# Twelve small products of attention's query and key norms, issued one by one between main products

## The chip, the core and the metric

The kernel runs on one core of a Trainium2 chip. Its time is what the device takes for one execution, in microseconds (us); the median of three runs before the change was 2003.21 us, the lowest 1998.88, the highest 2009.31.

The core's engines work side by side: TensorE (PE in the profile, its weight loads PEld) multiplies matrices, VectorE (DVE), ScalarE (ACT) and GpSimd (POOL) do the elementwise work, SyncE (SP) issues transfers. Each takes its instructions in the order of its own queue, and waits where it needs something that another has not finished.

## The reference

One layer of an encoder over 768 tokens (512 in a grid of 8 x 64, 256 in one of 4 x 64) of 2048 channels, in float32. Cut to what matters here:

```python
h = _rms(x, norm_g) * (1 + scl) + shift
proj = h @ w_in                      # 2048 x 10240
pool_u, pool_z, q, k, v, attn_z, g_pool, g_attn = split(proj)
pool_y = _pool_mixer(pool_u) * silu(pool_z)
q = _rms(q.reshape(B, S, 16, 64), q_norm_g)     # x * rsqrt(mean(x * x) + eps) * g, by head
k = _rms(k.reshape(B, S, 16, 64), k_norm_g)
attn_y = _neighbourhood_attention(q, k, v, rpb) * silu(attn_z)
merged = sigmoid(g_pool) * (pool_y @ w_pool_up) + sigmoid(g_attn) * (attn_y @ w_attn_up)
y = x + gate * (merged @ w_o)
```

The change is in the two lines for `q` and `k`: the sum of x * x over the 64 channels of each head, for every token.

## The kernel before, in words

**The main products.** Nearly all of TensorE's work is the projections. Channels lie on the partitions, tokens along the row. A weight and an operand are each split into a high and a low part, and one product becomes three main products in `steps`, line 493: high by high, high by low, low by high, each a load of 128 x 128 weights and 384 columns of the operand. A generator, `steps`, issues them; after every second weight tile (six main products) it calls `tick`. The parts of the weights (`whi` from ScalarE, `wlo` from VectorE) are made three pieces ahead.

**The small work by ticks.** Everything else is put on a calendar: `at(step, fn)` files a function under a tick, and `tick` calls what is due, so that its instructions stand in each engine's queue right behind the main products issued so far. Attention runs in eight pairs of heads, 42 ticks apart, beside the main products of the second half of the projection. A pair has six units of queries; a unit makes its scores `s` (tick 0), adds the bias on VectorE (1), exponentials on ScalarE (3), transposes the values (`vt`, 5) and the probabilities (`pt`, 9), splits these into parts (`ph` by ScalarE, `pl` by VectorE, 10), and multiplies (`op`, 13).

**The norms** (`norms`, from line 540) come ahead of a pair's first unit. ScalarE squares the pair's keys and queries (`sq`, line 550, two tiles of 128 x 768). TensorE sums the squares over each head's 64 channels (`n`, line 556): twelve instructions, six for the keys and six for the queries, each with 128 tokens' squares as weights and two columns of ones as its operand. The trace shows each as two passes, so 24 a pair. VectorE adds the epsilon (`nx`, 564), ScalarE takes logarithm and exponential (`ny`, 567 and 568), VectorE does a Newton step (`ny`, 574), TensorE spreads the result over the channels (`yk`, 592), and VectorE scales the keys. The tile of the sums, the scores and `yk` take turns in one PSUM buffer (the tag `s`).

Of the kernel before, what the change touches and what calls it, by code (L numbers as in the profile page):

```python
# [16 lines left out]
P = 128  # L17
# [34 lines left out]
def encoder_layer(ctx: ExitStack, tc: tile.TileContext, xT, cT, w_ada2, w_ada4, b_ada, norm_g, w_in, pool_w,  # L52
                  pool_scale, qg, kg, rpb, rcnt, w_pu, w_au, w_o, yT):
    nc = tc.nc
    pe, act, dve, pool, sp = nc.tensor, nc.scalar, nc.vector, nc.gpsimd, nc.sync
# [13 lines left out]
    def slot(name, dt=F32):  # L69
        heap["live"] += 1  # L70
        heap["peak"] = max(heap["peak"], heap["live"])
        assert heap["live"] <= SLOTS, (name, heap)
        return slab.tile([P, 2, TH], dt, tag="slot", name=name, bufs=SLOTS)

    def free(n=1):
        heap["live"] -= n
# [17 lines left out]
    def flat(t):  # L94
        return t.rearrange("p h n -> p (h n)")
# [6 lines left out]
    blk1 = const.tile([P, P], F32, name="blk1")  # L102
# [45 lines left out]
    def at(step, fn):  # L148
        plan.setdefault(max(step, clock["now"] + 1), []).append(fn)
# [2 lines left out]
        at(clock["now"] + n, fn)  # L152

    chores = []
    back = []
    pace = {"kind": "pair", "task": 0, "chore": 0, "back": 0}
    EVERY = {"plain": 1, "drop": 2, "pair": 3}
# [16 lines left out]
    def tick():  # L174
        clock["now"] += 1
        while plan.get(clock["now"]):
            plan[clock["now"]].pop(0)()
        pump()
# [152 lines left out]
    def need(st, op, j):  # L331
        hurry["on"] = True
        while (op, j) not in st.ops:
            if tasks and room() >= tasks[0][0] and tasks[0][1]():
                tasks.pop(0)[2]()
            elif back and room() >= back[0][0] and back[0][1]():
                back.pop(0)[2]()
            else:
                assert behind, (st.name, op, j, heap, len(tasks), len(back))
                flush()  # L340
        hurry["on"] = False
        if behind and behind["of"] is st.ops[op, j]:
            flush()
# [44 lines left out]
    def prepare(upto):  # L388
        load_more()
        while st_["split"] < min(len(seq), upto):  # L390
            split_next()
            load_more()

    def bank():
        return ps_acc.tile([P, 512], F32, tag="acc", name="acc", bufs=4)
# [80 lines left out]
    def steps():  # L476

        for i, s in enumerate(seq):
            prepare(i + 1 + st_["ahead"])
            c = s["c"]  # L480
            pace["kind"] = "plain" if s["kind"] == "plain" else "drop" if s["drop"] else "pair"
            if s["kind"] == "pair":
                stt, n = s["set"], s["n"]
                for j in range(n):
                    need(stt, s["op"], j)
                if s["first"]:
                    c[s["bank"]] = bank()
                out = c[s["bank"]][:, :TH]
                for j in range(n):
                    mh, ml = stt.mov(s["op"], j)  # L490
                    wh, wl = s["hi"][:, j, :], s["lo"][:, j, :]
                    for k, (w, m) in enumerate(((wh, mh), (wh, ml), (wl, mh))):
                        pe.matmul(out, w, m, start=s["first"] and j == 0 and k == 0, stop=j == n - 1 and k == 2,  # L493
                                  skip_group_check=True)
                    if j == n - 1:
                        if s["drop"]:
                            stt.drop(s["op"])
                        if s["hook"]:
                            s["hook"]()
                    if j % 2:  # L500
                        tick()
                        yield
            else:
                if s["begin"]:
                    c["ps"] = s["banks"]() if s["banks"] else [bank()[:, :TH] for _ in range(2)]
                for j in range(s["n"]):
                    mov = s["mov"](s["k0"] + j)
                    last = s["end"] and j == s["n"] - 1
                    for k, (w, m) in enumerate(((s["hi"], 0), (s["hi"], 1), (s["lo"], 0))):
                        for h in range(2):  # L510
                            pe.matmul(c["ps"][h], w[:, j, :], mov[h][m], start=s["begin"] and j == 0 and k == 0,  # L511
                                      stop=last and k == 2, skip_group_check=True)
                    if last:
                        s["hook"](c["ps"])
                    tick()
                    yield
# [3 lines left out]
    def run(n):  # L520
        if stream["gen"] is None:
            stream["gen"] = steps()
        for _ in range(n):
            next(stream["gen"])
# [15 lines left out]
    def norms(p, start):  # L540


        at_ = state["pool"]
        c = {}

        def squares():
            for nm in "kq":
                assert clock["now"] >= state["done", nm, p] + 5, (p, nm, clock["now"], state["done", nm, p])
                c["s" + nm] = slot("sq")
                act.activation(flat(c["s" + nm]), flat(state[nm, p]), AF.Square)  # L550

        def sums():
            n2 = ps_aux.tile([P, 2, 512], F32, tag="s", name="n2")[:, 0, :]
            for i, nm in enumerate("kq"):
                for u in range(6):
                    pe.matmul(n2[:, 12 * i + 2 * u : 12 * i + 2 * u + 2], flat(c["s" + nm])[:, P * u : P * (u + 1)],  # L556
                              blk1[:, 0:P:64], start=True, stop=True)
            free(2)
            c["n2"] = n2[:, :24]

        def take():
            c["x"] = at_.tile([P, 24], F32, tag="nx", name="nx", bufs=2)
            c["y"] = at_.tile([P, 24], F32, tag="ny", name="ny", bufs=2)
            dve.tensor_scalar(c["x"], c["n2"], 64 * EPS, None, op0=ALU.add)

        def root():
            act.activation(c["y"], c["x"], AF.Ln)
            act.activation(c["y"], c["y"], AF.Exp, scale=-0.5)

        def newton():  # L570
            x, y = c["x"], c["y"]
            dve.tensor_tensor(x, x, y, op=ALU.mult)
            dve.scalar_tensor_tensor(x, x, -0.5, y, op0=ALU.mult, op1=ALU.mult)
            dve.scalar_tensor_tensor(y, x, 1.5, y, op0=ALU.add, op1=ALU.mult)
            state["yq", p] = y[:, 12:24]

        def high(nm):
            c[nm + "h"] = slot(nm + "h", F32R)
            act.copy(flat(c[nm + "h"]), flat(state[nm, p]))

        def low(nm):
            c[nm + "l"] = slot(nm + "l", F32R)
            dve.tensor_tensor(flat(c[nm + "l"]), flat(state[nm, p]), flat(c[nm + "h"]).bitcast(F32), op=ALU.subtract)
            free()
            state["parts", p] = c

        def spread():
            c["b"] = ps_aux.tile([P, 2, 512], F32, tag="s", name="yk")
            for u in range(6):
                for h in range(2):  # L590
                    src = c["y"][:, 2 * u + h : 2 * u + h + 1].to_broadcast([P, 64])
                    pe.matmul(c["b"][HALF[h], u // 3, P * (u % 3) : P * (u % 3 + 1)], src, ident, start=True, stop=True)  # L592

        def scaled():
            k = state["k", p]
            dve.scalar_tensor_tensor(k, k, gqk, c["b"][:, :, :TH], op0=ALU.mult, op1=ALU.mult)

        for n, fn in ((0, squares), (2, sums), (3, take), (4, root), (4, lambda: high("q")), (5, newton), (6, spread),
                      (6, lambda: low("q")), (7, scaled), (8, lambda: high("k")), (9, lambda: low("k"))):
            at(start - 11 + n, fn)  # L600

    def attention(p, start, pace):
        at_ = state["pool"]
        vparts = {}
        norms(p, start)

        def unit_(u):
# [749 lines left out]
```

## Time and profile before

| | |
|---|---|
| median of three runs | 2003.21 us |
| profiled execution | 1998.88 us |
| its span, first to last instruction | 1997.1 us |
| TensorE busy (products / loads) | 1910.8 / 1805.7 us |
| VectorE, ScalarE, GpSimd busy | 1353.2, 1028.5, 375.6 us |
| mean granted clock of TensorE | 0.982 of full |

A time in the text without another unit is in us; moments are counted from the span's start. TensorE is busy for 96% of the span, and the chain of work that ended last runs through it for 83%. The clock of TensorE has two levels in the rows, 1.00 (2.4 GHz) and 0.50 (1.2 GHz). Matmuls overlap in the records, since each lasts until its last column is out: to see what one costs, count the time from one start to the next.

### The profile page before, as it was taken

The numbers are of one execution on the slowest core, as the hardware profiler recorded it, in microseconds if no ns is written. First come the engines' busy times: TensorE is split into PE (matmuls) and PEld (weight loads), VectorE is DVE, ScalarE is ACT, GpSimd is POOL, SyncE is SP. The second block draws the span as 40 slices with busy tenths as digits, with TensorE's granted clock in tenths as the row PEclk, the third lists the DMA queues.
The fourth block names the chain that finished last, engine by engine and source line by source line (L and its number), as shares of the span: only waits on it lengthen the run. The fifth ranks groups of instructions, "written<-read, shape, count | busy, mean of one in ns | idle before, by whom it ended". The sixth has DMA issues, their size and how long they took to land.

```text
span 1997.1 us, 31988 instructions
## 1 busy us (share of the span) xinstructions
PE 1910.8 (96%) x11752; PEld 1805.7 (90%) x11752; DVE 1353.2 (68%) x2422; ACT 1028.5 (52%) x2224; POOL 375.6 (19%) x593
## 2 busy tenths in 40 slices
PE   3899999999999999999999999999998999898998
PEld 2788989898999998999888898889998999897997
DVE  5755555666656578866867787677765779776654
ACT  4433334444444344546666666666554556565553
POOL 0000000111300146511111111111143022222211
PEclk9999999999999999999999999999999999999999
DMA  9755556777753555566555665556799589898865
GB/s 357 247 204 190 195 195 209 265 256 246 245 194 120 165 157 130 136 184 152 164 151 149 159 176 140 151 149 173 170 326 364 191 290 255 250 301 242 244 184 148
DMA packets 129678, 410.61 MB, mean 206 GB/s; under 512 B 16369, under 2 KB 21489, under 8 KB 129521
## 3 DMA queue, kind: packets, MB, share of 16 engines
q0 software_dynamic: 61408, 194.28, 35.9%
q1 hardware_dynamic: 67104, 214.20, 32.0%
q8 instruction: 92, 1.51, 0.3%
q14 instruction: 66, 0.53, 0.1%
q10 hardware_dynamic: 1008, 0.09, 0.0%
HBM read 290.54 MB, written 117.96 MB: 205 GB/s over the span
## 4 chain that ended last, share of the span: by engine, by line
PE 83%; DVE 5%; DMA 4%; issue 3%; ACT 3%; POOL 1%; SPq 0%; ACTq 0%; POOLq 0%; DVEq 0%
PE acc L493 73%; PE adaacc L530 2%; PE op L715 2%; PE acc L511 1%; DVE wlo L382 1%; PE n L556 1%; DMA adaw<-in_w_ada_dram 1%; PE s L621 1%; PE pt L682 1%; DMA xrB<-xrB 1%; PE yk L592 1%; DVE wsum L405 0%; DMA merged_d<-o 0%; DMA mbB<-mbB 0%; ACT o L435 0%
## 5 line engine op out<-in xcount | busy, mean ns | idle before, releaser
L382 DVE TENSOR_TENSOR wlo<-wraw,whi 128x512 fp32r<-128x512 f32 (+1 forms) x352 | 244.0, 694 | 287.4 <-ACT whi L381 285.6
L382 DVE TENSOR_TENSOR wlo<-wsum,whi 128x512 fp32r<-128x512 f32 x440 | 315.3, 717 | 129.4 <-ACT whi L381 122.6
L381 ACT CAST whi<-wsum 128x512 fp32r<-128x512 f32 x440 | 272.9, 620 | 166.5 <-ACT whi L381 55.7
L493 PE MATMUL acc<-xbT,whi 128*128 128x384 f32 x1280 | 346.5, 352 | 4.5 <-ACT u L420 4.5
L493 PE MATMUL acc<-xaT,whi 128*128 128x384 f32 x1216 | 313.3, 338 | 0.5 <-DVE xaT L204 0.5
L381 ACT CAST whi<-wraw 128x512 fp32r<-128x512 f32 (+1 forms) x352 | 213.0, 606 | 89.7 <-PE acc L493 69.6
L493 PE MATMUL acc<-xbB,whi 128*128 128x384 f32 x960 | 251.0, 342 | 1.7 <-DVE o L839 1.7
L420 ACT COPY u<-acc 128x384 f32<-128x384 f32 x220 | 105.2, 478 | 285.1 <-PE acc L493 285.0
L493 PEld LDWEIGHTS acc<-xbT,whi 128*128 128x128 f32 x1280 | 231.2, 194 | 12.9 <-ACT u L420 6.5
L493 PE MATMUL acc<-xaB,whi 128*128 128x384 f32 x912 | 235.2, 338 | 0.0
L493 PEld LDWEIGHTS acc<-xaT,whi 128*128 128x128 f32 x1216 | 217.7, 188 | 15.3 <-issue 14.4
L493 PE MATMUL acc<-xbT,wlo 128*128 128x384 f32 x640 | 219.6, 343 | 0.2 <-DVE wlo L382 0.2
L493 PE MATMUL acc<-xaT,wlo 128*128 128x384 f32 x608 | 203.7, 335 | 0.0
L493 PEld LDWEIGHTS acc<-xbB,whi 128*128 128x128 f32 x960 | 169.1, 188 | 8.2 <-ACT o L914 2.0
L493 PEld LDWEIGHTS acc<-xaB,whi 128*128 128x128 f32 x912 | 163.1, 188 | 11.9 <-issue 9.9
L493 PE MATMUL acc<-xbB,wlo 128*128 128x384 f32 x480 | 161.1, 336 | 0.0
L493 PE MATMUL acc<-xaB,wlo 128*128 128x384 f32 x456 | 152.8, 335 | 0.0
L405 DVE TENSOR_TENSOR wsum<-wraw 128x512 f32<-128x512 f32 x220 | 152.5, 693 | 0.2 <-DMA wraw<-in_w_in_dram 0.2
L405 DVE TENSOR_TENSOR wsum<-wsum,wraw 128x512 f32<-128x512 f32 x220 | 151.3, 688 | 0.2
L493 PEld LDWEIGHTS acc<-xbT,wlo 128*128 128x128 f32 x640 | 123.9, 194 | 0.5 <-DVE wlo L382 0.5
L435 ACT ACTIVATE o<-acc 128x384 f32<-128x384 f32 x110 | 54.1, 492 | 128.1 <-PE acc L493 127.7
L852 POOL DMA_DIRECT2D part_d<-o x76 | 41.2, 542 | 397.9 <-ACT o L435 323.1
(244 smaller groups left out, 3558.2 us busy)
## 6 DMA issues: line engine op xcount, KB each, us to landing
wraw<-in_w_in_dram SPq DMA_DIRECT2D x160, 512.0 KB, 4.6
adaw<-in_w_ada_dram SPq DMA_DIRECT2D x96, 512.0 KB, 5.9
part_d<-o POOLq DMA_DIRECT2D x116, 384.0 KB, 3.9
wraw<-in_w_o_dram SPq DMA_DIRECT2D x32, 512.0 KB, 6.6
o<-part_d POOLq DMA_DIRECT2D x40, 384.0 KB, 4.8
xbT<-xbT POOLq DMA_DIRECT2D x32, 384.0 KB, 5.6
xrT<-xrT POOLq DMA_DIRECT2D x32, 384.0 KB, 7.4
xyT<-xyT POOLq DMA_DIRECT2D x32, 384.0 KB, 8.0
```

The costliest lines, as they stand in the source:

```text
L381: act.copy(hi[:, :n, :], raw)
L382: dve.tensor_tensor(lo[:, :n, :], raw, hi[:, :n, :].bitcast(F32), op=ALU.subtract)
L405: dve.tensor_tensor(t[:, :n, :], a, b, op=ALU.add)
L420: act.copy(t, c["a"][:, :TH])
L435: act.activation(c["o2"][:, 0, :], c["a"][:, :TH], AF.Copy, scale=-1.0)
L493: pe.matmul(out, w, m, start=s["first"] and j == 0 and k == 0, stop=j == n - 1 and k == 2, skip_group_check=True)
L511: pe.matmul(c["ps"][h], w[:, j, :], mov[h][m], start=s["begin"] and j == 0 and k == 0, stop=last and k == 2, skip_group_check=True)
L530: pe.matmul(acc[32 * j : 32 * (j + 1), :n], cs[:, kt, :], w[:, n * j : n * (j + 1)], start=kt == 0, stop=kt == KT - 1)
L556: pe.matmul(n2[:, 12 * i + 2 * u : 12 * i + 2 * u + 2], flat(c["s" + nm])[:, P * u : P * (u + 1)], blk1[:, 0:P:64], start=True, stop=True)
L592: pe.matmul(c["b"][HALF[h], u // 3, P * (u % 3) : P * (u % 3 + 1)], src, ident, start=True, stop=True)
L715: pe.matmul(op[:, :256], a, b, start=i == 0, stop=i == len(prods) - 1)
L852: pool.dma_start(part_d[f], flat(t))
```

## The change

The block of twelve instructions is broken up. `sums` no longer issues them: it files them in a list, `small`, and `steps` takes one from it behind the first and one behind the third of every three main products, until the list is empty. Six weight tiles, that is three ticks, use up the twelve. So that the results are there at the same tick as before, the squares and the sums begin three ticks earlier (14 ahead of the pair's first unit for the squares, 11 before), and `take`, `root`, `newton` and what follows stay at the tick they had. A new step, `summed`, gives the two slots of the squares back.

```diff
     chores = []
+    small = []
     back = []
...
                     for k, (w, m) in enumerate(((wh, mh), (wh, ml), (wl, mh))):
                         pe.matmul(out, w, m, start=s["first"] and j == 0 and k == 0, stop=j == n - 1 and k == 2,
                                   skip_group_check=True)
+                        if small and k != 1:
+                            small.pop(0)()
...
         def sums():
             n2 = ps_aux.tile([P, 2, 512], F32, tag="s", name="n2")[:, 0, :]
-            for i, nm in enumerate("kq"):
-                for u in range(6):
-                    pe.matmul(n2[:, 12 * i + 2 * u : 12 * i + 2 * u + 2], flat(c["s" + nm])[:, P * u : P * (u + 1)],
-                              blk1[:, 0:P:64], start=True, stop=True)
+            c["n2"] = n2[:, :24]
+
+            def one(i, nm, u):
+                pe.matmul(n2[:, 12 * i + 2 * u : 12 * i + 2 * u + 2], flat(c["s" + nm])[:, P * u : P * (u + 1)],
+                          blk1[:, 0:P:64], start=True, stop=True)
+
+            small.extend(lambda i=i, nm=nm, u=u: one(i, nm, u) for i, nm in enumerate("kq") for u in range(6))
+
+        def summed():
+            assert not small
             free(2)
-            c["n2"] = n2[:, :24]
...
-        for n, fn in ((0, squares), (2, sums), (3, take), (4, root), (4, lambda: high("q")), (5, newton), (6, spread),
-                      (6, lambda: low("q")), (7, scaled), (8, lambda: high("k")), (9, lambda: low("k"))):
-            at(start - 11 + n, fn)
+        for n, fn in ((0, squares), (2, sums), (6, summed), (6, take), (7, root), (7, lambda: high("q")), (8, newton), (9, spread),
+                      (9, lambda: low("q")), (10, scaled), (11, lambda: high("k")), (12, lambda: low("k"))):
+            at(start - 14 + n, fn)
```

On TensorE, around the sums of the third pair, this stood in the order before, from the transposes of one unit to the first main products behind the block (`xbT`, `xbB` are operands, the number is the buffer's):

```order
L682 MATMUL pt<-ident,p 128x128 x2
L682 MATMUL pt<-ident,p 64x128 x2
L493 MATMUL acc<-xbT_7088,whi 128x384 x2
L493 MATMUL acc<-xbT_7088,wlo 128x384
...
L493 MATMUL acc<-xbB_7153,whi 128x384 x2
L493 MATMUL acc<-xbB_7153,wlo 128x384
L660 MATMUL vt<-ident,o_9590 96x128
L660 MATMUL vt<-ident,o_9590 64x128
L556 MATMUL n_10538<-blk_84,sq 128x2 x12
L493 MATMUL acc<-xbT_5501,whi 128x384 x2
L493 MATMUL acc<-xbT_5501,wlo 128x384
```

And at the same place after it:

```order
L690 MATMUL pt<-ident,p 128x128 x2
L690 MATMUL pt<-ident,p 64x128 x2
L494 MATMUL acc<-xbT_7088,whi 128x384
L560 MATMUL n_10490<-blk_84,sq 128x2
L494 MATMUL acc<-xbT_7088,whi 128x384
L494 MATMUL acc<-xbT_7088,wlo 128x384
L560 MATMUL n_10490<-blk_84,sq 128x2
...
L494 MATMUL acc<-xbB_7153,wlo 128x384
L560 MATMUL n_10490<-blk_84,sq 128x2
L668 MATMUL vt<-ident,o_9590 96x128
L668 MATMUL vt<-ident,o_9590 64x128
L494 MATMUL acc<-xbT_5501,whi 128x384 x2
```

The block of twelve has gone from behind `vt`; the same eighteen main products between `pt` and `vt` now have one sum behind the first and one behind the third of each three.

On ScalarE, at the same place, before (`o<-op` ends one unit, `p`, `u` and `o<-acc` take a main product out of PSUM):

```order
L723 COPY o<-op 64x128 x2
L420 COPY p_10462<-acc 128x384
L381 CAST whi<-wsum 128x512
L200 CAST xrT_10486<-in 128x384
L435 ACTIVATE o_10420<-acc 128x384
L695 CAST ph<-pt 128x256
L695 CAST ph<-pt 64x256
L698 CAST ph<-pt 64x256
L640 ACTIVATE p,sm<-p,mx 128x160 x2
L550 ACTIVATE sq<-o_10136 128x768
L550 ACTIVATE sq<-o_10169 128x768
L381 CAST whi<-wraw 128x512
```

And after:

```order
L731 COPY o<-op 64x128 x2
L553 ACTIVATE sq<-o_10136 128x768
L553 ACTIVATE sq<-o_10169 128x768
L421 COPY p_10466<-acc 128x384
L382 CAST whi<-wsum 128x512
L201 CAST xrT_10491<-in 128x384
L436 ACTIVATE o_10420<-acc 128x384
L703 CAST ph<-pt 128x256
L703 CAST ph<-pt 64x256
L706 CAST ph<-pt 64x256
L648 ACTIVATE p,sm<-p,mx 128x160 x2
L382 CAST whi<-wraw 128x512
```

The two squares stand ahead of eight instructions that they followed. The orders on VectorE, GpSimd and SyncE are the same as before, buffer numbers aside.

## Rows read from the trace of the kernel before

**Rows 1.** The page, parts 1 and 4: busy time, and the chain that ended last.

```profile
PE 1910.8 (96%) x11752; PEld 1805.7 (90%) x11752; DVE 1353.2 (68%) x2422; ACT 1028.5 (52%) x2224; POOL 375.6 (19%) x593
...
PE 83%; DVE 5%; DMA 4%; issue 3%; ACT 3%; POOL 1%; SPq 0%; ACTq 0%; POOLq 0%; DVEq 0%
```

**Rows 2.** Stretches at low clock behind the sums: length, busy times, clock, DMA.

```profile
881.52:884.93 3.41, 3.41 (x13) 3.41 (x12) 1.02 (x4) 1.00 (x2) 0.56 (x1) 0.50 0.98 214
...
sum 40.94, PE 40.94 PEld 36.94 DVE 14.44 ACT 14.88 POOL 7.82; mean PE 5.12 PEld 4.62 DVE 1.81 ACT 1.86 POOL 0.98
```

**Rows 3.** Timeline of TensorE, first pair: start, length, line, operation, count.

```profile
874.07 0.51 PE L493 MATMUL acc<-xbT,whi 128*128 128x384 f32 x2
...
877.54 0.33 PE L493 MATMUL acc<-xbB,wlo 128*128 128x384 f32 x1
877.71 2.74 PE L556 MATMUL n<-blk,sq 128*128 128x2 f32 x24
880.31 0.59 PE L493 MATMUL acc<-xbT,whi 128*128 128x384 f32 x2
880.74 0.33 PE L493 MATMUL acc<-xbT,wlo 128*128 128x384 f32 x1
...
882.31 0.84 PE L493 MATMUL acc<-xbT,whi 128*128 128x384 f32 x2
...
884.87 0.37 PE L493 MATMUL acc<-xbT,wlo 128*128 128x384 f32 x1
```

**Rows 4.** TensorE's waits, 875 to 1345: total, times, longest.

```profile
PE n L556 <- ACT sq L550: 3.0, 7, 0.4
...
PE yk L592 <- DVE ny L574: 0.5, 2, 0.2
```

**Rows 5.** Timeline of TensorE, third pair; in brackets the idle time before.

```profile
1000.19 0.60 PE L682 MATMUL pt<-ident,p 128*128 128x128 f32 x4
...
1003.59 0.34 PE L493 MATMUL acc<-xbB,wlo 128*128 128x384 f32 x1
1004.19 0.40 PE L660 MATMUL vt<-ident,o 128*96 128x128 f32 x2 [0.27 <-DVE pl L700]
1005.01 2.84 PE L556 MATMUL n<-blk,sq 128*128 128x2 f32 x24 [0.42 <-ACT sq L550]
1007.71 0.90 PE L493 MATMUL acc<-xbT,whi 128*128 128x384 f32 x2
```

**Rows 6.** A stretch ahead of the seventh block, main products (line 493) alone.

```profile
1267.22:1270.64 3.42, 1.55 (x9) 1.23 (x8) 1.00 0.89 188
```

**Rows 7.** Timeline of TensorE, a single transpose between main products.

```profile
917.49 0.34 PE L493 MATMUL acc<-xbB,wlo 128*128 128x384 f32 x1
917.66 0.27 PE L660 MATMUL vt<-ident,o 128*128 128x128 f32 x1
...
918.12 0.34 PE L493 MATMUL acc<-xbT,wlo 128*128 128x384 f32 x1
```

**Rows 8.** Timeline of ScalarE, third pair.

```profile
997.65 0.53 ACT L723 COPY o<-op 64x128 f32<-64x128 f32 x2
999.35 0.48 ACT L420 COPY p<-acc 128x384 f32<-128x384 f32 x1 [1.17 <-PE acc L493]
...
1001.88 0.49 ACT L435 ACTIVATE o<-acc 128x384 f32<-128x384 f32 x1 [1.12 <-PE acc L493]
...
1004.13 1.56 ACT L550 ACTIVATE sq<-o 128x768 f32<-128x768 f32 x2
```

**Rows 9.** Timeline of VectorE, third pair.

```profile
998.82 0.67 DVE L630 SCALAR_TENSOR_TENSOR p<-s,ny,bias 128x160 f32<-128x160 f32 x2
...
1003.30 0.75 DVE L700 TENSOR_TENSOR pl<-pt,ph 128x256 fp32r<-128x256 f32 x2 [2.23 <-ACT ph L698]
```

**Rows 10.** Timeline of TensorE, third pair, later.

```profile
1015.13 0.60 PE L682 MATMUL pt<-ident,p 128*96 128x128 f32 x4
1015.98 1.53 PE L592 MATMUL yk<-ident,ny 128*64 128x128 f32 x24 [0.25 <-DVE ny L574]
```

**Rows 11.** The sums (line 556) of the eighth pair at low clock.

```profile
1338.90:1340.48 1.58, 1.58 (x9) 1.58 (x8) 0.50 0.00 0
```

## The prediction, made before the changed kernel ran

> **What bounds the kernel now.** I read the page first. TensorE is busy for 96% of the span and holds 83% of the chain that ended last [rows 1], so a change is worth what it does to TensorE's own time. The line of clock digits on the page shows nothing here, because each digit covers 50 us; so next I asked for the work on the tile `n`, which the change moves, and then for the granted clock in short stretches around it. There are eight such blocks, one for each pair of heads, and behind every one of them the clock falls to 0.50, its lower level of 1.2 GHz: 40.94 us in all [rows 2]. The timeline of the first pair shows it closely [rows 3]: main products up to 877.54, then 24 passes of the sums (12 instructions of two passes each) up to 880.31, main products again, and from 881.5 on the same main products take twice as long. TensorE was never idle there. What stood before the fall was 2.6 us in which it mostly loaded weights and streamed two columns a pass.
>
> The seven later pairs also wait at this place: 0.42 us each for the squares from ScalarE [rows 4, 5], and just before it for the transposes `vt` [rows 5].
>
> **Term 1, the clock.** At the full level a main product takes (877.54 - 874.07) / 20 = 0.1735 us, at the lower one (884.87 - 882.31) / 8 = 0.320 us [rows 3]. A microsecond at the lower level thus does 0.54 us of work and loses 0.46. Over 40.94 us that is 18.8 us lost [rows 2]. If no fall comes after the change, all of it is gained; if the falls stay, nothing. I take 18.8. My reason is what stands in the new order: the longest stretch with no main product is one sum, two passes of 0.112 us, against 2.6 us before. The nearest row of before for so thin a mixture is 1267.2 to 1270.6, where only 1.55 us of main products (9 of them) ran beside waits and a few sums, at a clock of 1.00 throughout [rows 6]. In the new stretch 18 main products stand beside 12 sums: 18 x 0.1735 + 12 x 0.223 = 5.8 us, so about 10.6 main products in 3.4 us, a little denser than that row.
>
> The Trainium skill (TensorE: Matmul & The Clock Gate, "Why this matters for your kernels") puts drops of the clock down to gaps in which TensorE is idle between bursts, and advises to avoid these. By that alone a block in which TensorE is busy all the time would cost no clock, and spreading it would save only the waits, with the sum of the second case below. The trace does not agree: TensorE is 100% busy before each of the eight falls [rows 2, 3].
>
> **Term 2, the sums themselves.** Nothing is taken away: 12 instructions with 24 loads a pair before and after. In the block of the first pair the way from the main product at 877.54 to the third after it, at 880.74, is 3.20 us; three main products are 0.52, so the 24 passes cost 2.68 us, 0.112 each [rows 3]. That is the load's pace; the first load hides under the main product before it, and the next main product's load is exposed behind the last pass instead. The question is what a sum costs alone between two main products. The nearest row is a single transpose, one pass with a load of the same size: 0.63 us from 917.49 to 918.12, where three main products would be 0.52, so 0.11 [rows 7]. One pass alone costs what one in the block costs, and a sum alone should cost 2 x 0.112 = 0.223. I take a difference of zero. At one end, the second main product behind the block comes 0.26 us after the first (880.74 less 0.17 less 880.31) instead of 0.17 [rows 3]; if those 0.086 us were a price of each return and came 12 times instead of once, the loss would be 0.086 x 11 x 8 = 7.6 us. At the other end, one of the two loads could also hide under a main product: 0.112 x 12 x 8 = 10.7 us gained.
>
> The Trainium skill (TensorE: Matmul & The Clock Gate, Part 2, step 1) says that TensorE pulls weight loads ahead of matmuls in flight. Spread loads have long matmuls to hide under, so read freely it speaks for that gain of 10.7 us; the single transpose, whose row still shows the full 0.11 us, speaks against it, and the row decides my choice.
>
> **Term 3, the waits.** In the third pair the way from the last main product before the block (1003.59) to the first behind it (1007.71) is 4.12 us [rows 5]. Without waits it is 2.77 (first pair, 877.54 to 880.31 [rows 3]) and two transposes at 0.11 [rows 7], so 2.99. The difference is 1.13 us, in seven pairs 7.9 us. What becomes of it:
> - The squares. They now stand ahead of the copy of `p`, three steps earlier, right behind the two copies of `o<-op`. In the third pair these ended at 998.2 and ScalarE then idled 1.17 us before `p` and 1.12 us before the evacuation at 1001.88 [rows 8]. Two squares take 1.56 us; they would end at 999.8, and the first sum stands behind the four transposes that begin at 1000.19 [rows 5] and one main product, near 1000.7. The wait of 0.42 us should go. Queued behind the squares are the copy of `p` (some 0.4 us later), two casts and the evacuation, which the idle 1.12 us cover.
> - The PSUM tile `n` shares its buffer with the scores, and is now taken three steps earlier, so the first sum must wait for VectorE to have read the fourth unit's scores: 998.82 + 0.67 = 999.5 [rows 9], 1.2 us ahead of 1000.7. No wait.
> - `vt` waits for VectorE's `pl`, which ended at 1004.05 [rows 9], 2.17 us after the evacuation at 1001.88 that starts its chain [rows 8]. TensorE now has 12 main products and nine sums between the main product that releases that evacuation and `vt`: 2.08 + 2.01 = 4.09 us, where it had 2.08. This wait should go with about 1.7 us to spare.
> - What comes late next: the products of `yk` wait for `ny` from VectorE. They do so now in two pairs of eight, 0.25 us idle in the third pair [rows 4, 10], where the clock was back when the chain began; from the transposes at 1015.13 to `yk` at 1015.98 it is 0.85 us where four transposes need about 0.44. In the other later pairs the low clock hid that. I charge five more pairs 0.4 us: 2.0 us. The scores of the last unit, which need `n` read, have about 0.5 us of room by my count of the orders; if that fails it is up to 0.5 us a pair, 3.5 us.
> Between 0 and 7.9 I take 7.9 gained and 2.0 lost.
>
> On the DMA side nothing moves: the orders on SyncE and GpSimd are as before, and keys and queries have been on their way for ten steps at least when the squares now need them.
>
> **The sum.** 18.8 + 0 + 7.9 - 2.0 = 24.7 us. The profiled execution took 1998.88 us (its span is 1997.1, with 1.8 around it), so it would take 1974. It was the fastest of the three runs; the median, 2003.21, stands 4.3 us higher and would come to 1978.5. A kernel without eight falls should scatter less, so I put the forecast at **1977 us**.
>
> **Rivals.**
> 1. *The falls stay.* The new stretch is still half weight loads, and denser than its nearest row only by 10.6 main products to 9. Then only the waits go: 2003.2 - 7.9 = 1995. For it: all eight blocks drew a fall, however they lay. Against it: [rows 6]. Chance 0.13.
> 2. *Each return to a main product costs 0.086 us.* 1977 + 7.6 = 1985. For it: the second main product behind the block [rows 3]. Against it: the single transpose, which pays it once already within its 0.11 [rows 7]. Chance 0.09.
> 3. *Half of the loads hide.* 1977 - 10.7 = 1966. Chance 0.03.
> 4. *Slower: the low clock covers the longer stretch.* If the clock falls at the start of the mixture and stays down through it, 18 main products at 0.320 and 24 passes at 0.2 (1.58 us for about eight, [rows 11]) take 10.6 us instead of 5.8, and the 3.4 us behind it lose 0.46 of their time, 1.6 us: 6.4 us a pair where 18.8 / 8 = 2.35 are lost now. That is 8 x 4.05 = 32 us more, less 7.9 for the waits: 2003.2 + 24 = 2027. It decides from the point at which the low stretches come to more than about 58 us in all, since then term 1 is a loss that the waits no longer cover. Chance 0.05.
> That the change doesn't do what it says is out: the new order has one sum between main products, twelve times in each pair.
> The forecast keeps 0.70.
>
> **Range and chances.** The forecast's own range is 1970 to 1988: `yk` and the scores may wait 5 us more, and the waits at `vt` may stay in part. With the other cases it is 1966 to 1996, which leaves out the slower rival and little else. A measurement of this kernel tells about 0.5% from no change, here 10 us: faster means under 1993. Faster: nearly all of the forecast (0.68), rivals 2 and 3: 0.80. Within 0.5%: rival 1 and the rest: 0.14. Slower: 0.06.
>
> **What would show it.** Right: a clock of 1.00 in every stretch of 3 us from 875 to 1,400 us; single sums in the timeline with 0.40 us from the main product before to the one behind; no wait of the sums for the squares; and the same sum of TensorE passes. Term 1 is wrong if rows at 0.50 remain behind the sums. Term 2 is wrong if the stretch from the first sum to the last takes more than 6.2 or less than 5.2 us. Term 3 is wrong if `vt`, `yk` or the scores wait longer in all pairs than in the third now.

## The result, and the profile after

The changed kernel took **1980.75 us** (median of four runs, 1974.41 to 1982.72) against 2001.05 us before (four runs, 1996.25 to 2009.31): a ratio of **0.989, with a 95% interval of 0.987 to 0.991**. The forecast was 1977 us, with a range of 1966 to 1996. The profiled execution took 1981.33 us, with a span of 1979.6.

The page, answering to [rows 1]: TensorE is busy 12.8 us less with as many instructions.

```profile
PE 1898.0 (96%) x11752; PEld 1797.4 (91%) x11752; DVE 1353.0 (68%) x2422; ACT 1029.0 (52%) x2224; POOL 375.5 (19%) x593
...
PE 81%; DVE 7%; ACT 4%; DMA 4%; issue 3%; POOL 1%; ACTq 0%; POOLq 0%; DVEq 0%
```

The stretches from the first sum of a pair to its last, with the main products between (columns as in [rows 2]: stretch, its length, busy times of the five engines, clock, DMA). The whole of attention is the last row.

```profile
876.60:882.35 5.75, 5.75 (x43) 5.75 (x43) 1.99 (x3) 2.34 (x6) 1.42 (x2) 1.00 0.51 107
...
997.44:1003.29 5.85, 5.85 (x46) 5.85 (x43) 2.98 (x6) 3.54 (x12) 0.88 (x1) 1.00 0.40 65
1060.49:1067.11 6.62, 6.08 (x46) 5.85 (x43) 4.29 (x10) 4.83 (x14) 0.88 (x1) 1.00 0.37 60
...
870.00:1330.00 460.00, 451.42 (x2917) 417.84 (x2916) 350.46 (x733) 312.25 (x828) 64.35 (x90) 1.00 0.63 162
```

Where [rows 2] had 40.94 us at a clock of 0.50, the trace has no stretch at 0.50 between 860 and 1400 us. Seven stretches take 5.75 to 5.85 us, where the forecast had 5.8; the fourth takes 6.62. The timeline of TensorE in the third pair answers to [rows 3 and 5]:

```profile
997.09 0.60 PE L690 MATMUL pt<-ident,p 128*128 128x128 f32 x4
997.44 0.42 PE L494 MATMUL acc<-xbT,whi 128*128 128x384 f32 x1
997.71 0.28 PE L560 MATMUL n<-blk,sq 128*128 128x2 f32 x2
997.84 0.42 PE L494 MATMUL acc<-xbT,whi 128*128 128x384 f32 x1
...
1003.15 0.28 PE L560 MATMUL n<-blk,sq 128*128 128x2 f32 x2
1003.29 0.40 PE L668 MATMUL vt<-ident,o 128*96 128x128 f32 x2
1003.44 0.42 PE L494 MATMUL acc<-xbT,whi 128*128 128x384 f32 x1
...
1009.40 0.60 PE L690 MATMUL pt<-ident,p 128*96 128x128 f32 x4
1010.35 0.87 PE L600 MATMUL yk<-ident,ny 128*64 128x128 f32 x12 [0.35 <-DVE ny L582]
```

From the main product before a sum to the one behind it, 997.44 to 997.84, it is 0.40 us, as forecast. Neither the sums nor `vt` wait any more at this place; `yk` does. ScalarE, answering to [rows 8], has its two squares in what was its idle time, and the evacuation behind them still comes after 1.38 us idle:

```profile
994.51 0.53 ACT L731 COPY o<-op 64x128 f32<-64x128 f32 x2
995.06 1.58 ACT L553 ACTIVATE sq<-o 128x768 f32<-128x768 f32 x2
996.67 0.48 ACT L421 COPY p<-acc 128x384 f32<-128x384 f32 x1
...
999.45 0.49 ACT L436 ACTIVATE o<-acc 128x384 f32<-128x384 f32 x1 [1.38 <-PE acc L494]
```

TensorE's waits from 870 to 1330, answering to [rows 4] (the eight at `vt` for `pl` all lie elsewhere in the pairs; at this place none is left):

```profile
PE vt L668 <- DVE pl L708: 4.2, 8, 1.0
PE yk L600 <- DVE ny L582: 2.3, 7, 0.4
PE vt L668 <- PE acc L494: 1.3, 6, 0.2
PE n L560 <- DVE p L638: 0.5, 1, 0.5
```

To compare kernels I use the time from the first pair's `yk` to the last pair's, which holds seven of the eight pairs' sums. Each kernel's tile view gives it as the first and last start; before, then after:

```profile
L592 PE MATMUL yk<-ident,ny x192: 272/273/324, 886.2 to 1350.5; 128*64 128x128 f32 x192
```

```profile
L600 PE MATMUL yk<-ident,ny x192: 272/273/323, 886.9 to 1329.5; 128*64 128x128 f32 x192
```

This is 464.3 us before and 442.6 after: **21.7 us less**. The two profiled executions differ by 17.5 us, since the first `yk` comes 0.7 us later in the changed kernel and what follows the last one takes 3.5 us longer.

### The profile page after: what moved, and what is told of

Its sections match the earlier page's. It is cut to its first block, busy times and chain, and to the rows that moved or that the text cites. A ratio compares the mean times of both kernels' runs of the same rounds, so it can differ in the third digit from the quotient of the medians.

```text
span 1979.6 us, 32012 instructions
## 1 busy us (share of the span) xinstructions
PE 1898.0 (96%) x11752; PEld 1797.4 (91%) x11752; DVE 1353.0 (68%) x2422; ACT 1029.0 (52%) x2224; POOL 375.5 (19%) x593
## 4 chain that ended last, share of the span: by engine, by line
PE 81%; DVE 7%; ACT 4%; DMA 4%; issue 3%; POOL 1%; ACTq 0%; POOLq 0%; DVEq 0%
PE acc L494 72%; PE adaacc L533 2%; DVE wlo L383 2%; PE acc L514 2%; PE op L723 1%; DMA adaw<-in_w_ada_dram 1%; PE s L629 1%; ACT whi L382 1%; PE pt L690 1%; DVE sumsq L1103 1%; DMA xyT<-xyT 1%; DMA xrB<-xrB 1%; PE yk L600 1%; DVE wsum L406 1%; DVE p L638 1%
## 5 line engine op out<-in xcount | busy, mean ns | idle before, releaser
L494 PE MATMUL acc<-xbT,whi 128*128 128x384 f32 x1280 | 341.6, 346 | 4.6 <-ACT u L421 4.6
L494 PE MATMUL acc<-xbB,whi 128*128 128x384 f32 x960 | 261.2, 348 | 2.1 <-DVE o L847 1.7
L494 PEld LDWEIGHTS acc<-xbT,whi 128*128 128x128 f32 x1280 | 225.2, 189 | 12.2 <-ACT u L421 6.5
L494 PE MATMUL acc<-xbT,wlo 128*128 128x384 f32 x640 | 215.3, 336 | 0.2 <-DVE wlo L383 0.2
```

## Experiments

Each ran on the chip beside the kernel before. "yk to yk" is the time just named, "falls" counts the pairs at whose sums the clock fell in the one profiled execution, inside the block or behind it, with the time at 0.50 between 860 and 1400 us.

| kernel | time, us | ratio to before (95%) | yk to yk | falls |
|---|---|---|---|---|
| before | 1999.29 to 2002.26 | | 464.3 | 8, 40.9 us |
| changed, run again | 1980.71 | 0.990 (0.989-0.992) | 442.7 | 0 |
| block early | 1993.28 | 0.995 (0.993-0.997) | 457.5 | 3, 10.2 us |
| wide block | 1990.35 | 0.993 (0.991-0.995) | 453.8 | 0 |
| three each | 1994.19 | 0.996 (0.994-0.998) | 456.0 | 3, 10.2 us |
| one each | 1982.37 | 0.989 (0.985-0.992) | 447.6 | 1, 6.8 us |
| one pass | 1982.61 | 0.991 (0.990-0.993) | 439.1 | 0 |
| one tick later | 1978.78 | 0.989 (0.988-0.990) | 440.4 | 0 |
| squares early | 1991.93 | 0.995 (0.994-0.997) | 453.9 | 7, 27.3 us |
| block early, yk late | 1989.57 | 0.995 (0.994-0.997) | 455.3 | 7, 27.3 us |
| early chain | 1975.66 | 0.988 (0.987-0.989) | 439.5 | 0 |
| one pass, early chain | 1968.55 | 0.984 (0.983-0.985) | 432.6 | 0 |

**Is it the columns that stream?** The kernel before, block and order unchanged, each sum with 128 columns.

```diff
-pe.matmul(n2[:, 12 * i + 2 * u : 12 * i + 2 * u + 2], sq, blk1[:, 0:P:64], ...)
+m = 12 * i + 2 * u
+pe.matmul(n2[:, m : m + P].rearrange("p (n h) -> p n h", h=2), sq,
+          blk1.rearrange("p (h n) -> p n h", h=2), ...)
```

> The kernel before, with the block where it was, but each sum streams 128 columns (the two columns of ones over and over, the next sum writes over what is too much) instead of 2. Theory (columns): a pass still costs 0.112 us, since 128 columns take 0.053 and hide beside the next load; no fall behind the eight blocks; the waits of 7.9 us stay: 18 to 20 us faster than before, 1980 to 1984. Rival (what counts is that no main product stands between, or that these are float32 passes with a load each): all falls stay, 2000, or slower if the columns cost time: up to 0.053 x 24 x 8 = 10 us more.

Third pair of this kernel:

```profile
1000.69 0.40 PE L661 MATMUL vt<-ident,o 128*96 128x128 f32 x2 [0.27 <-DVE pl L701]
1001.51 3.56 PE L557 MATMUL n<-blk,sq 128*128 128x128 f32 x24 [0.42 <-ACT sq L550]
1004.79 0.62 PE L493 MATMUL acc<-xbT,whi 128*128 128x384 f32 x2
```

And the stretch behind its block, which has the clock at 1.00:

```profile
1004.80:1008.20 3.40, 3.40 (x21) 2.88 (x20) 0.88 (x4) 2.10 (x8) 0.84 (x1) 1.00 0.80 181
```

No fall is left in any pair, with the same block, the same loads and the same waits as in [rows 5]. The executions without a profile agree: the mean granted clock of the whole kernel was 0.988 to 0.992 in all seven, and 0.972 to 0.983 in the 22 of the kernel before beside them. So a want of streaming columns, and not the block, its loads or its type, drew the falls. The price was mis-sized: the block takes 3.28 us and not 2.70, 0.137 a pass. Against the theory, the 128 columns do not hide wholly beside the loads. In time it came to 1990, not 1980 to 1984. From this run the falls can be priced alone, over the seven pairs: 464.3 - 453.8 is 10.5 us gained, in spite of 0.58 x 7 = 4.1 us for the wider passes and 1.1 us more waiting at `yk` (1.6 against 0.5): 15.7 us, where 0.46 of the 37.5 us at low clock in these seven is 17.3.

**Is it only the earlier start?** The changed kernel's ticks, with the sums issued in one block.

```diff
-small.extend(lambda i=i, nm=nm, u=u: one(i, nm, u) for i, nm in enumerate("kq") for u in range(6))
+for i, nm in enumerate("kq"):
+    for u in range(6):
+        one(i, nm, u)
```

> The squares and the sums keep their new, earlier ticks, but the twelve sums stand in one block again. Theory (the clock falls because for over 2.5 us hardly a column streams; spreading mends that, moving mends the waits): the clock is at 0.50 behind each of the eight blocks again, 34 to 48 us in all, while the waits of the sums for the squares and of vt behind them are gone. About 8 us faster than before, 1991 to 1995. Rival (the gain comes from starting three ticks earlier): no fall, about 1981, like the changed kernel.

The second pair shows a fall at the end of such a block, with no wait ahead of it, and the third pair the wait at `yk`:

```profile
931.48 2.97 PE L560 MATMUL n<-blk,sq 128*128 128x2 f32 x24
934.31 0.99 PE L494 MATMUL acc<-xbT,whi 128*128 128x384 f32 x2
935.10 0.52 PE L494 MATMUL acc<-xbT,wlo 128*128 128x384 f32 x1
...
1010.90 0.60 PE L692 MATMUL pt<-ident,p 128*96 128x128 f32 x4
1012.78 1.42 PE L602 MATMUL yk<-ident,ny 128*64 128x128 f32 x22 [1.29 <-DVE ny L584]
```

The stretch of the second pair at low clock, in the columns of [rows 2]:

```profile
933.83:937.24 3.41, 3.41 (x13) 3.41 (x13) 0.00 (x0) 0.62 (x2) 0.00 (x0) 0.50 0.00 0
```

The kernel's waits from 870 to 1345, the first two rows:

```profile
PE yk L602 <- DVE ny L584: 8.8, 8, 1.3
PE vt L670 <- DVE pl L710: 5.3, 12, 1.0
```

The time lies in the range expected, but not for the reason given. Only three pairs drew a fall instead of eight, though in an execution whose mean granted clock, 0.990, was the highest of ten (the others had 0.983 to 0.988), so three may be fewer than is usual for this kernel. The wait for the squares is gone, as the theory had it; the one at `vt` is left in four of the seven pairs, 0.26 us each (12 waits listed, 8 in the changed kernel, 15 before), and `yk` waits 8.8 us where it waited 0.5 before. Rival and theory are both wrong in part: starting earlier moves the waits, and does not take them away.

**What if yk comes later?** The same with `yk`, `scaled` and `high` of the keys one tick later.

```diff
-(9, spread), ... (10, scaled), (11, lambda: high("k"))
+(10, spread), ... (11, scaled), (12, lambda: high("k"))
```

> The block at the earlier ticks in one piece, as in the first experiment, and yk with what follows it one tick later. Theory (against the spread sums, the early block loses by the 8.8 us that yk waits and by some falls): the waits at yk fall below 2 us, two to five falls stay, so 6 to 8 us faster than the first experiment, 1984 to 1988, and still 3 to 7 us slower than the changed kernel. Rival (the wait moves on to the scores behind yk): no gain, 1991 to 1995.

The waits at `yk` fell from 8.8 to 0.9 us, and yet yk to yk gained only 2.2. This time seven of the same blocks drew a fall, 27.3 us instead of 10.2. One of them comes before the first `yk`; the others have 13.7 us more than the three had, and 0.46 x 13.7 = 6.3 us went that way. The time, 1989.57 us, missed the 1984 to 1988 expected. A bare block of 2.7 us thus draws a fall in some executions and pairs and not in others; what decides was not settled.

**The squares alone early.** The kernel before, with `(-3, squares)` instead of `(0, squares)`.

> The kernel before, with the squares alone three ticks earlier; the block stands where it stood, behind vt. Theory (what draws a fall is the length of the stretch in which hardly anything streams: waits, vt and block together): the wait for the squares goes (3.0 us idle), that for vt stays; the stretch gets shorter from 4.1 to some 3.5 us, falls stay behind six to eight pairs, mostly shorter: 20 to 38 us at the lower level, 1990 to 1998. Rival (the waits alone draw the falls): few or none, under 10 us at the lower level, 1983 to 1987.

```profile
1008.27 0.40 PE L660 MATMUL vt<-ident,o 128*96 128x128 f32 x2 [0.27 <-DVE pl L700]
1008.50 3.30 PE L556 MATMUL n<-blk,sq 128*128 128x2 f32 x24
1011.67 0.99 PE L493 MATMUL acc<-xbT,whi 128*128 128x384 f32 x2
```

In the third pair `vt` still waits, the sums no longer do, and the clock falls within the block. Seven falls, 27.3 us: as the theory had it, and against the rival, as far as a run can tell that leaves the waits at `vt` in place. The profiled execution took 1997.62 us, 5.7 above the median. Taking the wait for the squares away saves time by itself, but mends the clock only in part.

**How thin may the mixture be?** Three sums behind every main product, then one.

```diff
-if small and k != 1:
-    small.pop(0)()
+for _ in range(3):          # the other kernel: if small: small.pop(0)()
+    if small:
+        small.pop(0)()
```

> As the changed kernel, but three sums behind every main product, so that the twelve are used up within four main products and 12 x 0.223 + 4 x 0.1735 = 3.4 us. Theory: too little streams there, the clock falls behind most pairs (five to eight of eight), 1988 to 1995. Rival (any main product in between keeps the clock up): no fall, 1979 to 1983.

> As the changed kernel, but a sum behind every main product: twelve in twelve main products and 4.8 us. Theory: in between; I expect at most three falls, 1978 to 1986. If it falls behind most pairs, two of three is close to the thickest mixture that holds the clock, and the time is 1988 to 1995. Rival (any main product in between is enough): no fall, and the same time as the changed kernel within 2 us.

Three each: three falls, fewer than expected, and 7.2 us of waits at `yk`. One each: a single fall, in the fourth pair, where the first sum had waited 0.58 us for the buffer, and 4.0 us of waits at `yk`. The rival (any main product in between is enough) falls with the first. With two of three, the changed kernel and four variants of it showed no fall in six profiles of eight pairs, the fourth pair's wait included.

**What does a pass cost?** One pass a sum, squares and ones in float32r; this rounds the squares.

```diff
-c["s" + nm] = slot("sq")
+c["s" + nm] = slot("sq", F32R)
...
+two = const.tile([P, 2], F32R, name="two")
+act.copy(two, blk1[:, 0:P:64])
```

> As the changed kernel, but squares and ones are stored as float32r, so that a sum is one pass with one load in place of two (the squares are rounded to that type). Theory (each pass between main products costs its load, 0.112 us): the stretch from the first sum to the last takes 18 x 0.1735 + 12 x 0.112 = 4.5 us in place of 5.84, 1.34 us a pair and 10.7 in all; up to 0.4 us a pair may come back as waits at vt and yk, so 7.5 to 10.7 us faster than the changed kernel, 1970 to 1974. Rival (one of the two loads hides under a main product anyway): under 1 us, 1979 to 1982.

```profile
1000.93 0.42 PE L496 MATMUL acc<-xbT,whi 128*128 128x384 f32 x1
1001.19 0.17 PE L562 MATMUL n<-two,sq 128*128 128x2 f32 x1
...
1005.41 0.40 PE L670 MATMUL vt<-ident,o 128*96 128x128 f32 x2
...
1011.62 0.60 PE L692 MATMUL pt<-ident,p 128*96 128x128 f32 x4
1013.49 0.77 PE L602 MATMUL yk<-ident,ny 128*64 128x128 f32 x10 [1.26 <-DVE ny L584]
```

The stretch takes 4.48 us (1000.93 to 1005.41), 1.37 less than the changed kernel's 5.85: each pass taken away gives back 0.114 us, where the theory had 0.112. But the time was not the 1970 to 1974 expected; none was gained. `yk` now waits 1.26 us in this pair and 8.0 us in all, which leaves 3.5 us yk to yk. And the start of the kernel took some 5 us longer than in the changed one: the copy of the ones had been put ahead of all other work of ScalarE, and its first activation for the kernel proper came at 15.5 us instead of 7.3.

**The short chain behind the sums.** First the sums and `yk` a tick later each; then, instead, `take`, `root` and `newton` a tick earlier; then this with one pass, and the copy of the ones just ahead of attention.

```diff
-(2, sums), (6, summed), (6, take), (7, root), (7, lambda: high("q")), (8, newton), (9, spread)
+(3, sums), (6, summed), (6, take), (7, root), (7, lambda: high("q")), (8, newton), (10, spread)   # first
+(2, sums), (5, summed), (5, take), (6, root), (7, lambda: high("q")), (7, newton), (9, spread)    # second, third
```

> As the changed kernel, but the sums begin one tick later, and yk with what follows it stands one tick later. Theory (the waits left at this place come from short chains): the fourth pair's wait of 0.78 us for the PSUM buffer goes, and the 1.9 us at yk fall below 0.5: 2 to 3 us less between the first yk and the last, 1976 to 1980, which a measurement of the time hardly tells. Rival (the waits move on to the scores, which wait for the scaled keys): the same total, with over 1.5 us at the scores.

> The changed kernel with take, root and the Newton step one tick earlier, sums as they are (two passes). Theory: the waits at yk (2 us in all) go, the fourth pair's wait for the buffer stays; 1.5 to 2.5 us less in attention, 1977 to 1981, no difference that a measurement can tell. Rival (the earlier take delays the splits of vt behind it on VectorE): new waits of over 1 us at op or vt, same time or slower.

> One pass a sum (squares rounded to float32r), with take and root one tick earlier and the Newton step one tick earlier too; the copy of the two columns of ones stands just ahead of attention, not at the start. Theory (a pass less saves 0.112 us; what came back was the wait at yk, 9 us, because the chain from the sums to ny hung behind other work on ScalarE and VectorE): the wait at yk falls under 1 us, and the stretch of attention is 10 to 13 us shorter than the changed kernel's: 1967 to 1973. Rival (the wait goes elsewhere: vt, scores): over 5 us of it there, 1974 to 1980.

With the sums and `yk` later, the fourth pair's wait and those at `yk` are gone, 2.2 us yk to yk. With the earlier chain it is 3.1 us, and the time, 1975.66 us, came out below the 1977 to 1981 expected; its waits from 870 to 1345 no longer name `yk`:

```profile
PE vt L668 <- DVE pl L708: 4.2, 8, 1.0
PE vt L668 <- PE acc L494: 1.6, 7, 0.2
PE n L560 <- DVE p L638: 0.5, 1, 0.5
```

One pass with the earlier chain is the fastest version, 1968.55 us and 10.0 us less yk to yk than the changed kernel. Of the 8.0 us at `yk` 1.6 are left, where under 1 was expected:

```profile
PE yk L601 <- DVE p L639: 1.6, 4, 0.4
```

**The changed kernel again.**

> The changed kernel once more, unchanged, to see what of its profile repeats. Theory: no fall between 870 and 1330 us, six pairs with a wait at yk of 0.2 to 0.4 us, one wait of the sums (fourth pair); the longer falls near 36, 1490 and 1804 us, where the code is as before, vary by some microseconds from one execution to the next: 1978 to 1983. Rival (the change itself lengthens the later falls by some 3 us): again 10 us at the lower level near 1490 and 10 near 1804.

Time, waits and clock in attention came out as in the first profile. The stretches at low clock elsewhere differ from kernel to kernel where the code is the same: near 35 us from 3.4 to 13.7, and from 1480 to 1840 us from 17.1 to 27.3 in all. Before had 6.8 and 17.1, the changed kernel 13.7 and 27.3, and 13.7 and 23.9 when run again. Both ends of the later range also occur with the other arrangement (17.1 with one pass, 27.3 with the wide block), so neither theory is needed for it; a cost of the change of one or two us there is not excluded.

## Why the prediction was right, and where it was not

**Term 1, the clock: right.** All eight falls went, as forecast, and the wide block shows why: with the block left whole but more columns streaming, they go too. Its size was 18.8 us by the two rates of a main product; for the seven pairs that the wide block prices, 15.7 us stand against 17.3. The comparison with the row ahead of the seventh block [rows 6] carried the choice between "all" and "nothing", and it held, but the margin was not large: one sum behind every main product drew a fall once, three each drew three.

**Rival 1** (the falls stay, 1995) is out. So are idle gaps as their cause: in the wide block the same waits stand and no fall follows, and in the early block the second pair's clock falls with no wait ahead. The kernel before shows this in one pair only. The prediction says that TensorE was 100% busy before each of the eight falls, but [rows 2] shows it busy during them. Only the first pair's block has no wait ahead [rows 3]; the seven others stand behind 0.27 and 0.42 us of idle time, as in [rows 5]. In three of them the clock fell inside the block and not behind it (in the second pair at 939.54, with the block from 937.57 to 940.95). By the rule of the Trainium skill (TensorE: Matmul & The Clock Gate, "Why this matters for your kernels") nothing but the waits would have been saved; the measurement decides against it here.

**Term 2, the sums: right.** A pass between main products costs what it costs in the block, 0.112 to 0.114 us: 5.84 us for the stretch where 5.80 was worked out, and 1.37 us less with twelve passes fewer. Rivals 2 and 3 (a price for each return, hidden loads) are out by the same rows. Hidden loads were what the Trainium skill (TensorE: Matmul & The Clock Gate, Part 2, step 1), read freely, spoke for.

**Term 3, the waits: right in kind, with one miss.** The squares no longer hold up the sums, and `vt` no longer waits in this place. The block at the early ticks shows what the nine sums between the evacuation and `vt` did: without them `vt` waits again in four of the seven pairs. The miss is the PSUM buffer. I worked it out for the third pair alone, with 1.2 us of room [rows 9], and wrote "no wait". The fourth pair has two more operations on VectorE ahead of the bias, and its first sum waited:

```profile
1060.49 0.42 PE L494 MATMUL acc<-xbT,whi 128*128 128x384 f32 x1
1061.45 0.35 PE L560 MATMUL n<-blk,sq 128*128 128x2 f32 x2 [0.54 <-DVE p L638]
```

That cost 6.62 - 5.84 = 0.8 us. For `yk` 2.0 us were charged; its idle time rose from 0.5 to 2.3, 1.8 us.

**The sum.** Yk to yk, for seven pairs: 17.3 for the clock, 7.9 less 0.8 for the waits, less 1.8 at `yk`, gives 22.6, or 21.0 with the wide block's 15.7; measured are 21.7. The profiled execution came out 7 us above the 1974 worked out for it. Of these, 1.5 lie yk to yk (23.2 forecast for seven pairs), 2.3 ahead of the first `yk` (the first pair's fall should have given 1.6, and it came 0.7 later) and 3.5 behind the last; in these two places, outside the changed code, the changed kernel had the longer stretches at low clock. The median came out 2 us above 1978.5. The mechanism was right; the execution taken for the sum seems to have been lucky elsewhere, with 6.8 and 17.1 us at low clock where other profiles go up to 13.7 and 27.3, but with one profile of the kernel before, that is not shown.

**The slower rival** (the clock stays down through the mixture): out, with no fall in any stretch of two of three.

## What to carry to other kernels

An engine that is 100% busy can still be losing time. If many narrow matmuls stand together, look at the granted clock just behind them, and mix them between wide ones, or let them stream more columns, before anything else about them is tuned. A block that goes also took time in which other engines caught up: work out the chains around it in every repetition, not in one, and move the next chain up by as much.

## What the runs showed of the hardware that was not expected

A float32 pass with 128 x 128 weights took 0.112 us with two columns and 0.137 with 128 columns, though a third of a main product's 384 columns streams in 0.1735 / 3 = 0.058 (the main products are of the type float32r; no run times the streaming of a float32 pass by itself). And a bare block of 24 two-column passes, 2.7 us long, drew a fall of the clock in three pairs of eight in one kernel and seven of eight in another with the same block, one profile of each, where the kernel before, with waits and transposes ahead of it, had eight of eight.
